# A two-layer diffusion backbone on one core: Fourier tables made first, and part of the adaLN of layer 0 moved from TensorE to VectorE

## The chip, the cores and the metric

The kernel runs on one core of one Trainium2 chip. A core has a matrix engine (TensorE, PE in the profile), VectorE (DVE), ScalarE (ACT), GpSimd (POOL) and SyncE (SP), which issues most DMAs. The metric is device time in microseconds for one execution; of several runs the median is given.

## What is computed

Two layers over 256 latent tokens and 256 context tokens with 1024 channels, all in float32. Layer 0 mixes tokens with a Conformer convolution module, layer 1 with a bidirectional mLSTM; each is followed by a squared-ReLU MLP. What concerns the change is the adaLN map, which makes shift, scale and gate vectors from the conditioning vectors, and the convolution module:

```python
sh1, sc1, g1, sh2, sc2, g2 = jnp.split(jax.nn.silu(c) @ ada_w[i] + ada_b[i], 6, axis=-1)   # and so for c_ctx
u = h * (1 + sc1) + sh1
a = u @ w_pw1 + b_pw1
a = a[..., :CONV_DIM] * jax.nn.sigmoid(a[..., CONV_DIM:])
a = dwconv(a, w_dw)                       # 31 taps; rows of 64 for the latent tokens
a = jax.nn.silu(layer_norm(a + b_dw, ln_g, ln_b))
y = a @ w_pw2 + b_pw2
h = layer_norm(ALPHA * h + g1 * y, ln1_g, ln1_b)
h = layer_norm(ALPHA * h + g2 * mlp(h * (1 + sc2) + sh2), ln2_g, ln2_b)
```

## The kernel before

Every float32 product is made of three matmuls of split halves: a weight is cast by ACT to a high part `wh` (line 154) and DVE subtracts it from the raw weight to get the low part `wl` (line 155); PE then does `wh*xh` (L177), `wh*xl` (L180) and `wl*xh` (L181). Weights come as 1 MB loads into `raw`, which has three buffers, all issued by SP in one queue. A PSUM tile named `mm` has three buffers, `cv` and `ln` two, `fl` one.

The order of instructions in each engine's queue is set by a scheduler when the program is built, from the order of the code and its own costs; only the start loop is pinned (`pin[0]`): there PE's instructions keep the order of the code.

The stages up to the first MLP:

- Start (`start0`, `start1`, `start2`): for each of 8 channel tiles, one load of the part of `ada_w` that makes shift and scale, a tile of `x` and a tile of pw1's weights. PE multiplies the conditioning vectors with the load (`ada_mm`, L297, into `fl`), DVE copies the result (L532), PE folds four partial sums (L305, into `ln`), DVE makes `sh1` and `sc1` (L537, L538), ACT and DVE make `u`, and PE adds this channel tile's share to the first four output tiles of pw1.
- Fourier tables: the depthwise convolution is done by products with cosine and sine tables `tab`, made by DVE with a polynomial (L583 to L600), then by PE with the 31 taps (L622) into `Hc` and `Hs`. In the code this stands behind the start loop; the scratch tiles `F` (five buffers) are shared with it.
- pw1: two output tiles for each group of weights (`gemm`), 24 matmuls each. Behind each tile `pw1_epi` takes the sigmoid on ACT, the gated product `E` on DVE (L673), four transposes on PE (L676) and a copy to `A` on ACT. After four channel tiles a pass of `spectral` follows (L691 or L696, then products with `Hc` and `Hs` on DVE, then L716), and so at the end.
- adaLN of layer 0: `Ada` makes the other vectors in units of 512 columns. One unit has two 1 MB loads and 8 matmuls (shown as 16 pieces of L297). Units 4 and 5 (g1) run beside pw1, units 6 to 9 (sh2 and sc2) behind it, units 10 and 11 (g2) in the MLP. `AdaRows` makes the vectors of layer 1 otherwise: DVE multiplies 128 rows of the transposed map with the conditioning vector `cb`, broadcast to all partitions, and sums each row (L357). It runs in the MLP of layer 0.
- `token_norm`: statistics, an inverse root by four Newton steps on one column (13 small DVE instructions), and two DVE passes, for each of four token tiles. `silu` then transposes (L775) and makes the input of pw2 for one stream; stream 0 is the context.

Of the kernel before, what the change touches and what calls it, by code (L numbers as in the profile page):

```python
# [72 lines left out]
def hybrid_kernel(ctx: ExitStack, tc: tile.TileContext, xT, vecs_d, cc_d, rows_d, wdw_d, ada0_w, ada_w, ada1_w, wg_d, pw1a, pw1, pw2, w1_0, w2_0,  # L73
# [216 lines left out]
    for i in range(2):  # L290
        nc.vector.tensor_tensor(cs[:, :, 14 + i], sgc[:, i * DT:(i + 1) * DT], cc[:, i * DT:(i + 1) * DT], op=ALU.mult)
    ada = [con.tile([P, 48, 2], F32, name=f"ada{l}") for l in range(2)]
# [48 lines left out]
    class AdaRows:  # L341

        def __init__(self, first, last):
            self.m, self.last = first, last

        def step(self):
            m = self.m
            if m == self.last:
                return
            self.m += 1  # L350
            if m % 2 == 0:
                self.raw = raw_load(ada1_w[m // 2])
            w = self.raw[:, m % 2 * D:(m % 2 + 1) * D]
            o = _OFF["ada_b1"][0] + m
            for s in range(2) if m < 2 * DT else (1,):
                dump = w if s else tp.tile([P, D], BF16, tag="F", name=nm("dump"), bufs=1)
                nc.vector.tensor_tensor_reduce(dump, w, cb[:, s, :], 1.0, vecs[:, o:o + 1], ALU.mult, ALU.add,  # L357
                                               accum_out=ada[1][:, m, s:s + 1])

        def flush(self):  # L360
            while self.m < self.last:
                self.step()
# [23 lines left out]
    HALVES_D = [slice(0, 512), slice(512, D)]  # L386
# [90 lines left out]
    def rsqrt(r, v, q):  # L477


        nc.vector.tensor_scalar(v, v, EPS, None, op0=ALU.add)  # L480
# [29 lines left out]
    U = maker(qa, "u", 3 * DT)  # L510
    padp = open_pool("pads")
    F = maker(padp, "F", 5)

    x, u = [], []
    KO0 = 4
    ps0 = [psum("cv" if m == 3 else "mm") for m in range(KO0)]
    sc1 = con.tile([P, 2, DT], F32, name="sc1p")
    sh1 = con.tile([P, 2, DT], F32, name="sh1p")
    o0 = _OFF["ada_b0"][0]
    st = {}  # L520

    def start0(f):
        t = X()
        raw = raw_load(ada0_w[f])
        nc.sync.dma_start(t, xT[f * P:(f + 1) * P, :])
        wr = F()
        nc.sync.dma_start(wr[:, :KO0 * P], pw1a[f])
        x.append(t)
        ps = psum("fl")[:, :2 * P]
        ada_mm(ps, [raw[:, kt * 2 * P:(kt + 1) * 2 * P] for kt in range(DT)])  # L530
        sb = F()[:, :2 * P]
        nc.vector.tensor_copy(sb, ps)  # L532
        st[f] = wr, sb

    def start1(f):
        tr = ada_fold(st[f][1], 2 * P, tag="ln")
        nc.vector.tensor_scalar(sh1[:, :, f], tr[:, 0:2], vecs[:, o0 + f:o0 + f + 1], None, op0=ALU.add)  # L537
        nc.vector.tensor_scalar(sc1[:, :, f], tr[:, 2:4], vecs[:, o0 + DT + f:o0 + DT + f + 1], 1.0,  # L538
                                op0=ALU.add, op1=ALU.add)
        u.append((U(F32R), U(F32R)))  # L540
        affine_split(*u[f], x[f], sc1, sh1, f)
        st[f] = split_w(st[f][0][:, 0:KO0 * P])

    def start2(f):
        for m in range(KO0):
            mm3(ps0[m], *kcol(st[f], m), *u[f], f == 0, f == DT - 1)

    pin[0] = Z.pin0
    for f in range(DT + 2):
        if 0 <= f - 1 < DT:  # L550
            start1(f - 1)
        if f < DT:
            start0(f)
        if f >= 2:
            start2(f - 2)
    pin[0] = False

# [55 lines left out]
    WIN = [[(F0[0:96, :], 0)], [(ge32, 0), (lt32, 1)], [(ge96, 0), (F0[0:96, :], 1)], [(ge32, 1)]]  # L613
    bdw = padp.tile([P, D], F32, name="bdw")
    nc.sync.dma_start(bdw, wdw_d[NTAP:NTAP + 1, :].broadcast_to([P, D]))
    Hc, Hs = [padp.tile([P, D], F32, name=n_) for n_ in ("Hc", "Hs")]
    for h_ in range(2):
        wd = F()[:NTAP, :]
        nc.sync.dma_start(wd, wdw_d[0:NTAP, h_ * 512:(h_ + 1) * 512])
        for t, w_ in ((Hc, WC), (Hs, WS)):  # L620
            ps = psum("ln")
            nc.tensor.matmul(ps, w_[:NTAP, :], wd, start=True, stop=True)  # L622
            nc.scalar.activation(t[:, h_ * 512:(h_ + 1) * 512], ps, AF.Identity, scale=cf)


# [34 lines left out]
    A = padp.tile([P, 4, D], F32, name="A")  # L660
    Y = [[U() for _ in range(2)] for _ in range(4)]
    bst = con.tile([P, 4, 2, 6], F32, name="bst")
    hold = {}

    def pw1_epi(m, ps):
        f, gate = m // 2, m % 2 == 0
        if gate:
            sg = tmp("E")
            nc.scalar.activation(sg, ps, AF.Sigmoid, bias=V("b_pw1", DT + f))
            hold[f] = sg  # L670
            return
        a = hold.pop(f)
        nc.vector.scalar_tensor_tensor(a, ps, V("b_pw1", f), a, op0=ALU.add, op1=ALU.mult)  # L673
        tr = psum("ln")
        for b in range(4):
            nc.tensor.transpose(tr[:, b * P:(b + 1) * P], a[:, b * P:(b + 1) * P], ident)  # L676
        nc.scalar.copy(A[:, :, f * P:(f + 1) * P], tr.rearrange("p (b c) -> p b c", b=4))
        if f % 4 == 3:
            for tt in range(4):
                spectral(f // 4, tt)  # L680

    def spectral(h, tt):

        sl = slice(h * 512, (h + 1) * 512)
        ps_ = []
        xfs = [psum() for _ in range(2)]
        for b in (1, 0):
            if tt < 2:
                w_ = WIN[2 * tt + b]
                for i, (fm, t) in enumerate(w_):  # L690
                    nc.tensor.matmul(xfs[b], fm, A[0:fm.shape[0], t, sl], start=i == 0, stop=i == len(w_) - 1)  # L691
            else:

                def fwd():
                    r = slice(64 * b, 64 * b + 64)
                    return nc.tensor.matmul(xfs[b], F0[r, :], A[r, tt, sl], start=True, stop=True,  # L696
                                            tile_position=(64 * b, 0))
                if b:
                    lead = fwd()
                else:  # L700
                    with tc.issue_after(lead.ins):
                        fwd()
        for xf in xfs[::-1]:
            p1, p2 = F(), F()
            nc.vector.tensor_tensor(p1, xf, Hc[:, sl], op=ALU.mult)
            nc.vector.tensor_tensor(p2, xf, Hs[:, sl], op=ALU.mult)
            ps_.insert(0, (p1, p2))


        o = psum("cv")  # L710
        for i, g_ in enumerate((G1, G2)):
            for b in (0, 1):
                r = 64 * b

                def inv():
                    return nc.tensor.matmul(o[r:r + 64, :], g_[:, r:r + 64], ps_[b][i], start=i == 0, stop=i == 1,  # L716
                                            tile_position=(0, r))
                if b == 0:
                    lead = inv()
                else:  # L720
                    with tc.issue_after(lead.ins):
                        inv()
        nc.vector.tensor_tensor(Y[tt][h], o, bdw[:, sl], op=ALU.add)
        nc.vector.bn_stats(bst[:, tt, h, :], Y[tt][h])
        if h == 1:
            token_norm(tt)

    def token_norm(tt):
        mv = con.tile([P, 4], F32, name=nm("mv"))
        nc.vector.bn_aggr(mv[:, 0:2], bst[:, tt].rearrange("p h c -> p (h c)"))  # L730
        ve, r, q = mv[:, 1:2], mv[:, 2:3], mv[:, 3:4]
        rsqrt(r, ve, q)
        nc.vector.scalar_tensor_tensor(q, mv[:, 0:1], -1.0, r, op0=ALU.mult, op1=ALU.mult)
        for h in range(2):
            nc.vector.tensor_scalar(Y[tt][h], Y[tt][h], r, q, op0=ALU.mult, op1=ALU.add)

    pre2 = {}

    def pre_pw2(g):
        raw = raw_load(pw2[g, 0])  # L740
        for m in (0, 1):
            pre2[2 * g + m] = split_w(raw[:, m * 1024:(m + 1) * 1024])

    for m in range(KO0):
        pw1_epi(m, ps0[m])
    ada_g1, ada_s2 = Ada(4, 2), Ada(6, 4)
# [39 lines left out]
    for _ in silu(0):  # L786
        pass
# [899 lines left out]
```

## Time and profile before

| | |
|---|---|
| Median of 3 runs | 1714.17 us (1712.07 to 1720.13) |
| The profiled execution | 1711.55 us, its span 1709.7 us |
| PE busy | 1678.7 us, 98% of the span |
| DVE busy | 1051.9 us, 62% |
| ACT busy | 734.1 us, 43% |
| Bytes moved by DMA | 301.65 MB, on average 176 GB/s |

The page is of one profiled execution; times in its views are microseconds from the start of the span. In rows of the timeline the two numbers are start and duration, and a bracket gives how long the engine had been idle and what ended that. In rows of groups they are count, busy time and mean, then idle time before. A matmul of 512 columns is shown longer than the time to the next, because matmuls are pipelined and their ends are modelled.

### The profile page before, as it was taken

How to read it: one execution, taken by the hardware profiler on the slowest of the kernel's cores; microseconds unless marked ns; L12 is line 12 of the kernel's file. 1: busy time of each engine (PE TensorE's matmuls, PEld its weight loads, DVE VectorE, ACT ScalarE, POOL GpSimd, SP SyncE). 2: the span in 40 equal slices, each digit the busy share in tenths (PEclk: the TensorE clock that was granted, in tenths of full speed). 3: DMA queues.
4: the chain of work that ended last, by engine and by line, in shares of the span. 5: the costliest groups of instructions: out<-in, count | busy, mean ns of one | idle time of the engine just before them, and what ended most of it. 6: DMA issues, size and time to landing. Idle time of an engine off the chain costs nothing.

```text
span 1709.7 us, 23961 instructions
## 1 busy us (share of the span) xinstructions
PE 1678.7 (98%) x9514; PEld 1401.4 (82%) x9514; DVE 1051.9 (62%) x1899; ACT 734.1 (43%) x1168; POOL 33.6 (2%) x84
## 2 busy tenths in 40 slices
PE   8999999999999999999999999999999999999998
PEld 5655798888888999987678899998867778888886
DVE  5556897975666786773132443343387786678765
ACT  3311763232324365543232433342276674555651
POOL 0000000000000000000000000000011110000000
PEclk9999999999999999999999999999999999999999
DMA  9323533655555145568663542353355555656651
GB/s 365 131 119 110 214 146 124 245 203 167 197 212 169 64 136 191 179 193 266 232 217 123 196 163 83 112 185 124 123 186 188 206 173 203 243 182 222 236 187 46
DMA packets 62687, 301.65 MB, mean 176 GB/s; under 512 B 8114, under 2 KB 22962, under 8 KB 29168
## 3 DMA queue, kind: packets, MB, share of 16 engines
q1 hardware_dynamic: 42832, 285.44, 47.3%
q10 hardware_dynamic: 19744, 14.69, 2.7%
q8 instruction: 75, 1.23, 0.3%
q14 instruction: 36, 0.29, 0.1%
HBM read 284.37 MB, written 15.74 MB: 176 GB/s over the span
## 4 chain that ended last, share of the span: by engine, by line
PE 87%; DVE 5%; DMA 4%; ACT 2%; issue 1%; POOL 0%; SPq 0%; DVEq 0%; ACTq 0%; POOLq 0%
PE mm L177 17%; PE mm L181 17%; PE mm L180 17%; DMA raw<-ada_w 3%; PE mm L187 3%; PE mm L185 3%; PE mm L1509 3%; PE mm L186 3%; PE cv L186 2%; PE cv L185 2%; PE cv L187 2%; PE mm L1510 2%; DVE wl L155 1%; PE fl L297 1%; PE fl L647 1%
## 5 line engine op out<-in xcount | busy, mean ns | idle before, releaser
L155 DVE TENSOR_TENSOR wl<-raw,wh 128x1024 fp32r<-128x1024 f32 x346 | 421.9, 1223 | 346.6 <-ACT wh L154 344.2
L154 ACT CAST wh<-raw 128x1024 fp32r<-128x1024 f32 x346 | 360.7, 1050 | 546.3 <-PE mm L180 350.1
L180 PE MATMUL mm<-u,wh 128*128 128x256 f32 (+1 forms) x1152 | 377.4, 328 | 0.0
L177 PE MATMUL mm<-u,wh 128*128 128x256 f32 (+1 forms) x1024 | 328.3, 321 | 5.8 <-DVE E L673 2.9
L181 PE MATMUL mm<-u,wl 128*128 128x256 f32 (+1 forms) x1024 | 327.3, 320 | 0.1
L180 PEld LDWEIGHTS mm<-u,wh 128*128 128x128 f32 x1152 | 220.6, 192 | 18.3 <-DVE mv L482 0.8
L177 PEld LDWEIGHTS mm<-u,wh 128*128 128x128 f32 x1024 | 196.3, 192 | 27.6 <-issue 8.9
L181 PEld LDWEIGHTS mm<-u,wl 128*128 128x128 f32 x1024 | 196.7, 192 | 15.8 <-DVE wl L155 1.6
L177 PE MATMUL mm<-xm,wh 128*128 128x512 f32 x256 | 102.8, 402 | 0.0
L185 PE MATMUL mm<-wh,xl 128*128 128x512 f32 x256 | 101.3, 397 | 0.7 <-ACT wh L154 0.5
L186 PE MATMUL mm<-wh,xl 128*128 128x512 f32 x256 | 100.4, 392 | 0.6 <-DVE xl L155 0.6
L181 PE MATMUL mm<-xm,wl 128*128 128x512 f32 x256 | 100.3, 392 | 0.0
L187 PE MATMUL mm<-wl,xl 128*128 128x512 f32 x256 | 99.7, 395 | 0.3 <-DVE wl L155 0.2
L177 PE MATMUL mm<-hid,wh 128*128 128x512 f32 (+1 forms) x256 | 93.3, 365 | 1.2 <-ACT hid L154 1.2
L180 PE MATMUL mm<-hid,wh 128*128 128x512 f32 (+1 forms) x256 | 93.0, 363 | 0.4 <-DVE hid L155 0.4
L181 PE MATMUL mm<-hid,wl 128*128 128x512 f32 (+1 forms) x256 | 92.9, 363 | 0.0
L357 DVE CUSTOM_DVE_ANT_0 raw<-raw,cb,vecs 128x1024 f32<-128x1024 f32 x48 | 61.1, 1281 | 33.5 <-DMA raw<-ada_w 33.2
L1509 PE MATMUL mm<-x,wh 128*128 128x512 f32 x224 | 79.0, 397 | 0.0
L180 PE MATMUL mm<-qq,wh 128*128 128x272 f32 x256 | 73.9, 289 | 0.0
L177 PE MATMUL mm<-qq,wh 128*128 128x272 f32 x256 | 73.9, 289 | 0.0
L181 PE MATMUL mm<-qq,wl 128*128 128x272 f32 x256 | 73.8, 288 | 0.0
L177 PEld LDWEIGHTS mm<-xm,wh 128*128 128x128 f32 x256 | 48.1, 188 | 22.5 <-issue 7.5
(481 smaller groups left out, 3102.4 us busy)
## 6 DMA issues: line engine op xcount, KB each, us to landing
raw<-w SPq DMA_DIRECT2D x64, 1024.0 KB, 4.9
raw<-ada_w SPq DMA_DIRECT2D x48, 1024.0 KB, 4.9
raw<-wo SPq DMA_DIRECT2D x32, 1024.0 KB, 4.8
raw<-wv SPq DMA_DIRECT2D x16, 1024.0 KB, 5.7
raw<-wqT SPq DMA_DIRECT2D x16, 1024.0 KB, 5.8
raw<-wq SPq DMA_DIRECT2D x16, 1024.0 KB, 5.1
raw<-wk SPq DMA_DIRECT2D x16, 1024.0 KB, 4.8
raw<-pw SPq DMA_DIRECT2D x10, 1024.0 KB, 6.5
```

The lines of the kernel that those rows point to most:

```text
L154: c = nc.scalar.copy(hi, src)
L155: nc.vector.tensor_tensor(lo, src, hi.bitcast(F32), op=ALU.subtract)
L177: a = nc.tensor.matmul(ps, wh, xh, start=start, stop=False)
L180: nc.tensor.matmul(ps, wh, xl, start=False, stop=False)
L181: nc.tensor.matmul(ps, wl, xh, start=False, stop=stop)
L185: nc.tensor.matmul(ps, xh, wh, start=start, stop=False)
L186: nc.tensor.matmul(ps, xl, wh, start=False, stop=False)
L187: nc.tensor.matmul(ps, xh, wl, start=False, stop=stop)
L297: a = nc.tensor.matmul(ps[32 * j:32 * j + 32], cs[:, kt, 14 - 2 * v:46 - 2 * v], blocks[kt], start=first and kt < 4, stop=last and kt >= 4 ...
L357: nc.vector.tensor_tensor_reduce(dump, w, cb[:, s, :], 1.0, vecs[:, o:o + 1], ALU.mult, ALU.add, accum_out=ada[1][:, m, s:s + 1])
L1509: a = lambda stop: nc.tensor.matmul(ps, wh, u2[kt], start=kt == 0, stop=stop)
L1510: b = lambda: nc.tensor.matmul(ps[:, LO], wl, u2[kt][:, LO], start=False, stop=False)
```

## The change

- The code of the Fourier tables stands ahead of the start loop. The taps' products (`taps`) are made in two halves, one early in pw1 and one at output tile 11 of pw1, into `Hcs` (four tiles of 512 columns instead of two of 1024).
- g1 and sc2 of layer 0 are made by `AdaRows(0, (2, 4))`: 16 column tiles of 128, two streams each, hence 32 row sums on DVE, one or two column tiles behind each pw1 tile. The units 4, 5, 8 and 9 of `Ada` go; units 6 and 7 (sh2) stay. The `ada_w` loads of these parts become loads of `adar_w`, the same bytes transposed.
- For the row sums `cb` is needed early. The two conditioning vectors, already on the chip as columns `cs`, are written to DRAM (`c_dr`) by two DMAs that ACT issues, and read back broadcast by SP. Before, `cb` was loaded from an input and passed through a sigmoid.
- `x` is scaled and `gb` added behind tile 5 of the loop instead of behind pw1.
- `token_norm` works on two token tiles: one inverse root of two columns, three Newton steps, and the norm is applied by ACT.
- In the second spectral pass the two context tiles, their norm, the first pw2 weights, the two remaining `Ada` units and `silu(0)` come ahead of the two latent tiles.
- `cb` and the later `hl` share one buffer, and the pool `adap` goes.

```diff
+    c_dr = dp.tile([2, D], F32, name="c_dr")
+    for i in range(2):
+        nc.scalar.dma_start(c_dr[i].rearrange("(f p) -> p f", p=P), cs[:, :, 14 + i])
...
+        def __init__(self, layer, parts):
+            self.l, self.todo = layer, [(layer * 6 + i) * DT + j for i in parts for j in range(DT)]
+
+        def step(self, n=1):
+            for _ in range(n):
+                if not self.todo:
+                    return
+                g = self.todo.pop(0)
+                if g % 2 == 0:
+                    self.raw = raw_load(adar_w[g // 2])
+                w, m = self.raw[:, g % 2 * D:(g % 2 + 1) * D], g - self.l * 6 * DT
+                o = _OFF[f"ada_b{self.l}"][0] + m
+                for s in range(2) if self.l == 0 or m < 2 * DT else (1,):
+                    dump = w if s else tp.tile([P, D], BF16, tag="F", name=nm("dump"), bufs=1)
+                    nc.vector.tensor_tensor_reduce(dump, w, cb[:, s, :], 1.0, vecs[:, o:o + 1], ALU.mult, ALU.add,
+                                                   accum_out=ada[self.l][:, m, s:s + 1])
...
-        nc.vector.tensor_scalar(v, v, 0.5, None, op0=ALU.mult)
-        for _ in range(4):
-            nc.vector.tensor_scalar(q, r, r, v, op0=ALU.mult, op1=ALU.mult)
+        for _ in range(3):
+            nc.vector.tensor_tensor(q, r, r, op=ALU.mult)
+            nc.vector.scalar_tensor_tensor(q, q, 0.5, v, op0=ALU.mult, op1=ALU.mult)
             nc.vector.scalar_tensor_tensor(r, q, -1.5, r, op0=ALU.add, op1=ALU.mult)
...
+    def token_norm(t0):
...
+        rsqrt(r, mv[:, :, 1], v, q)
+        nc.vector.tensor_tensor(z, mv[:, :, 0], r, op=ALU.mult)
+        nc.vector.tensor_scalar(r, r, -1.0, None, op0=ALU.mult)
+        for i in range(2):
+            for h in range(2):
+                y = Y[t0 + i][h]
+                nc.scalar.activation(y, y, AF.Identity, scale=r[:, i:i + 1], bias=z[:, i:i + 1])
...
-    ada_g1, ada_s2 = Ada(4, 2), Ada(6, 4)
+    ada0, ada_sh = AdaRows(0, (2, 4)), Ada(6, 2)
...
     def pw1_next(m, ps):
         pw1_epi(m + KO0, ps)
-        if m in Z.fd[:2]:
-            ada_g1.mm()
-        if m == Z.fd[2]:
-            ada_g1.end()
+        ada0.step(2 if m % 3 else 1)
+        if m == 5:
+            for s, sl in HALVES:
+                nc.vector.tensor_tensor(gb[:, s, :], ad(0, s, "g1"), VA("b_pw2"), op=ALU.mult)
+                for f in range(DT):
+                    nc.vector.tensor_scalar(x[f][:, sl], x[f][:, sl], ALPHA, gb[:, s, f:f + 1], op0=ALU.mult, op1=ALU.add)
+        if m == 7:
+            taps(1)
+
+    nc.sync.dma_start(cb, c_dr.rearrange("(o s) c -> o s c", o=1).broadcast_to([P, 2, D]))
...
-    gemm(pw1, range(6), u, T, pw1_next)
-    for g in range(2):
-        pre_pw2(g)
-    for i in range(4):
-        ada_s2.mm()
-    ada_s2.end()
+    for t0 in (0, 2):
+        for tt in (t0, t0 + 1):
+            spectral(1, tt)
+        token_norm(t0)
+        if t0 == 0:
+            for g in range(2):
+                pre_pw2(g)
+            for i in range(2):
+                ada_sh.mm()
+            ada_sh.end()
+            for _ in silu(0):
+                pass
```

What becomes of the queues shows best in three places. In each row stand the line, the operation, the tiles written and read with their numbers, and the shape.

First DVE at the start, around the copy of the first adaLN product out of `fl` (`fl_125` before, `fl_190` now). Before:

```order
L141 TENSOR_TENSOR fold<-fold,ident 128x16
L145 TENSOR_TENSOR foldg<-foldg,ident 128x16
L532 COPY F_134<-fl_125 128x256
L145 TENSOR_TENSOR foldg<-foldg,ident 128x16
L155 TENSOR_TENSOR wl_150<-F_123,wh_149 128x512
L145 TENSOR_TENSOR foldg<-foldg,ident 128x16
L537 TENSOR_SCALAR sh1p<-ln_136,vecs 128x2
```

The same place in the changed kernel, where `F_139`, `F_140`, `F_153` and `F_154` are the scratch tiles of the tables:

```order
L553 SCALAR_TENSOR_TENSOR F_139<-F_139,F_140 128x384
L550 TENSOR_TENSOR F_154<-tab 128x256
L554 SCALAR_TENSOR_TENSOR tab<-F_139,tab 128x384
L551 TENSOR_SCALAR F_153<-F_154 128x256
L586 COPY F_199<-fl_190 128x256
L553 SCALAR_TENSOR_TENSOR F_153<-F_153,F_154 128x256
L591 TENSOR_SCALAR sh1p<-ln_201,vecs 128x2
```

The copy stood behind small instructions on 16 columns; now nearly all of the table arithmetic stands ahead of it, and the rest between it and the instructions that follow.

Second DVE in the pw1 loop, up to the gated product of the second of two tiles ahead of the first spectral pass (`E_704`, now `E_715`). Before:

```order
L155 TENSOR_TENSOR wl_837<-raw_834,wh_836 128x1024
L673 SCALAR_TENSOR_TENSOR E_635<-mm_604,vecs,E_635 128x512
L155 TENSOR_TENSOR wl_867<-raw_834,wh_866 128x1024
L155 TENSOR_TENSOR wl_906<-raw_903,wh_905 128x1024
L673 SCALAR_TENSOR_TENSOR E_704<-mm_673,vecs,E_704 128x512
L155 TENSOR_TENSOR wl_950<-raw_903,wh_949 128x1024
```

Now, where an `ISA` row that reads `cb` is a row sum and the one behind it writes out its result:

```order
L155 TENSOR_TENSOR wl_846<-raw_843,wh_845 128x1024
L155 TENSOR_TENSOR wl_884<-raw_843,wh_883 128x1024
L360 ISA dump_877,ada_108<-raw_875,cb,vecs 128x1024
L360 ISA ada_108 128x1
L360 ISA raw_875,ada_108<-raw_875,cb,vecs 128x1024
L360 ISA ada_108 128x1
L360 ISA dump_880,ada_108<-raw_875,cb,vecs 128x1024
L360 ISA ada_108 128x1
L624 SCALAR_TENSOR_TENSOR E_715<-mm_684,vecs,E_715 128x512
```

Three row sums, on a load of their own (`raw_875`), now stand between the weights' low parts and the gated product.

Third PE behind the second spectral pass, where `cv` are the products of its last step, `u_576`, `u_578` (now `u_553`, `u_555`) the normalized context tokens and `fl_1290` the adaLN units. Before:

```order
L297 MATMUL fl_1290<-raw_1315,cs 32x512
L716 MATMUL cv_1247<-F_1243,tab 64x512
L716 MATMUL cv_1247<-F_1239,tab 64x512
L716 MATMUL cv_1247<-F_1244,tab 64x512
L716 MATMUL cv_1247<-F_1240,tab 64x512
L297 MATMUL fl_1290<-raw_1315,cs 32x512 x3
L775 MATMUL ln_1358<-ident,u_578 128x128
L775 MATMUL ln_1377<-ident,u_578 128x128
L297 MATMUL fl_1290<-raw_1317,cs 32x512 x4
```

Now:

```order
L667 MATMUL cv_1387<-F_1380,tab 64x512
L667 MATMUL cv_1406<-F_1402,tab 64x512
L667 MATMUL cv_1406<-F_1398,tab 64x512
L667 MATMUL cv_1406<-F_1403,tab 64x512
L667 MATMUL cv_1406<-F_1399,tab 64x512
L708 MATMUL ln_1299<-ident,u_553 128x128
L708 MATMUL ln_1318<-ident,u_553 128x128
L708 MATMUL ln_1299<-ident,u_555 128x128
```

The adaLN units no longer stand between the last spectral products and the context's transposes.

More of the change, by code (lines that the diff above doesn't have):

```diff
@@ L72, in hybrid_kernel @@
 @with_exitstack
[L73 removed]
+def hybrid_kernel(ctx: ExitStack, tc: tile.TileContext, xT, vecs_d, rows_d, wdw_d, ada0_w, ada_w, adar_w, wg_d, pw1a, pw1, pw2, w1_0, w2_0,
                   w1_1, w2_1, up_x, up_z, wv, wo, bo_d, wk, wq, wqT, wdown, out):
@@ L341, in hybrid_kernel @@
     class AdaRows:
[L343 to L358, printed above, removed]
+        def __init__(self, layer, parts):
[13 more added lines that the diff above has]
+                                                   accum_out=ada[self.l][:, m, s:s + 1])
         def flush(self):
-            while self.m < self.last:
-                self.step()
+            self.step(len(self.todo))
     def ad(l, s, which):
@@ L510, in hybrid_kernel @@
     U = maker(qa, "u", 3 * DT)
+    cb = xp.tile([P, 2 * D], F32, tag="hl", name="cb").rearrange("p (s c) -> p s c", s=2)
     padp = open_pool("pads")
     F = maker(padp, "F", 5)
[L514 to L556, printed above, removed]
     HL = L // 2
@@ L613, in hybrid_kernel, with start0 @@
     WIN = [[(F0[0:96, :], 0)], [(ge32, 0), (lt32, 1)], [(ge96, 0), (F0[0:96, :], 1)], [(ge32, 1)]]
+    x, u = [], []
+    KO0 = 4
+    ps0 = [psum("cv" if m == 3 else "mm") for m in range(KO0)]
+    sc1 = con.tile([P, 2, DT], F32, name="sc1p")
+    sh1 = con.tile([P, 2, DT], F32, name="sh1p")
+    o0 = _OFF["ada_b0"][0]
+    st = {}
+    def start0(f):
+        t = X()
+        raw = raw_load(ada0_w[f])
+        nc.sync.dma_start(t, xT[f * P:(f + 1) * P, :])
+        wr = F()
+        nc.sync.dma_start(wr[:, :KO0 * P], pw1a[f])
+        x.append(t)
+        ps = psum("fl")[:, :2 * P]
+        ada_mm(ps, [raw[:, kt * 2 * P:(kt + 1) * 2 * P] for kt in range(DT)])
+        sb = F()[:, :2 * P]
+        nc.vector.tensor_copy(sb, ps)
+        st[f] = wr, sb
@@ new lines, in hybrid_kernel, with pw1_epi @@
+    pin[0] = Z.pin0
+    for f in range(DT + 2):
+        if 0 <= f - 1 < DT:
+            start1(f - 1)
+        if f < DT:
+            start0(f)
+        if f >= 2:
+            start2(f - 2)
+    pin[0] = False
+    A = padp.tile([P, 4, D], F32, name="A")
+    Y = [[U() for _ in range(2)] for _ in range(4)]
+    bst = con.tile([P, 4, 2, 6], F32, name="bst")
+    hold = {}
+    def pw1_epi(m, ps):
+        f, gate = m // 2, m % 2 == 0
+        if gate:
+            sg = tmp("E")
+            nc.scalar.activation(sg, ps, AF.Sigmoid, bias=V("b_pw1", DT + f))
+            hold[f] = sg
+            return
+        a = hold.pop(f)
+        nc.vector.scalar_tensor_tensor(a, ps, V("b_pw1", f), a, op0=ALU.add, op1=ALU.mult)
+        tr = psum("ln")
+        for b in range(4):
+            nc.tensor.transpose(tr[:, b * P:(b + 1) * P], a[:, b * P:(b + 1) * P], ident)
+        nc.scalar.copy(A[:, :, f * P:(f + 1) * P], tr.rearrange("p (b c) -> p b c", b=4))
+        if f == 3:
+            for tt in range(4):
+                spectral(0, tt)
@@ L657, in wgq_step @@
                               qtr.rearrange("p (b j c) -> p j b c", b=4, j=4)[:, :, :, 0:16])
[L660 to L742, printed above, removed]
```

148 lines of the change are left out of this document (98 added, 50 removed).

## The prediction

> **What bounds the kernel now.** I read the page's engine table, then what TensorE waited for, then busy time by stretches of the first 300 us, because from the first MLP on both versions queue the same instructions in the same order.
>
> ```profile
> span 1709.7 us, 23961 instructions
> PE 1678.7 (98%) x9514; PEld 1401.4 (82%) x9514; DVE 1051.9 (62%) x1899; ACT 734.1 (43%) x1168; POOL 33.6 (2%) x84
> PE fl L297 <- DMA raw<-ada_w: 9.8, 4, 6.3
> PE mm L177 <- DVE E L673: 2.9, 1, 2.9
> ```
>
> TensorE (PE) is busy 98% of the span. A change can win only PE work taken out, PE waits removed (31 us in all), or stretches in which PE runs below its full clock; it loses wherever PE is made to wait. The two largest waits, in us, number of times and longest, lie where the change works. The stretches (span, busy us of PE, weight loads, VectorE (DVE), ScalarE (ACT), GpSimd; then granted PE clock, DMA share, GB/s):
>
> ```profile
> 0.00:10.00 10.00, 2.95 (x20) 1.61 (x20) 3.47 (x27) 3.88 (x8) 2.51 (x13) 1.00 0.82 311
> 47.30:83.30 36.00, 32.99 (x133) 22.18 (x131) 15.96 (x26) 12.14 (x16) 1.75 (x8) 0.91 0.33 120
> 170.00:180.00 10.00, 6.74 (x34) 2.07 (x34) 7.46 (x30) 2.08 (x5) 0.00 (x0) 1.00 0.89 352
> ```
>
> PE idles 7.05 us at the head, 3.0 us behind the Fourier tables, with the clock at 0.91 there, and 3.3 us at the end of the convolution.
>
> **Term A, tables in front: +6.8 us.** DVE's queue at the start and in the old place of the tables, then PE's at the start:
>
> ```profile
> 4.14 0.25 DVE L291 TENSOR_TENSOR cs<-sgc,vecs 128x8 f32<-128x8 f32 x2 [0.40 <-ACT sgc L289]
> 4.98 0.17 DVE L145 TENSOR_TENSOR foldg<-foldg,ident 128x16 f32<-128x16 f32 x1
> 8.28 0.43 DVE L532 COPY F<-fl 128x256 f32<-128x256 f32 x1 [3.13 <-PE fl L297]
> 9.81 0.22 DVE L537 TENSOR_SCALAR sh1p<-ln,vecs 128x2 f32<-128x2 f32 x1 [0.34 <-PE ln L305]
> 44.56 0.55 DVE L594 SCALAR_TENSOR_TENSOR F<-tab 128x384 f32<-128x384 f32 x1
> 50.24 0.28 DVE L597 TENSOR_SCALAR F<-F 128x256 f32<-128x256 f32 x1
> 52.09 0.41 DVE L599 SCALAR_TENSOR_TENSOR F<-F,F 128x256 f32<-128x256 f32 x1
> 6.29 1.93 PE L297 MATMUL fl<-raw,cs 128*32 128x256 f32 x16 [6.29 <-DMA raw<-ada_w]
> 8.76 1.01 PE L305 MATMUL ln<-fold,F 128*128 128x2 f32 x4 [0.54 <-DVE F L532]
> 13.96 1.93 PE L297 MATMUL fl<-raw,cs 128*32 128x256 f32 x16 [0.35 <-DMA raw<-ada_w]
> 15.83 0.80 PE L177 MATMUL mm<-u,wh 128*128 128x512 f32 x1
> ```
>
> From 44.56 to 50.24, the end of that instruction included, DVE does 17 instructions in 5.9 us, about 0.34 us each; the whole of the tables is about 10 us of DVE. DVE has 3.13 us free before the copy of the first adaLN result at 8.28, and its new queue puts some 30 instructions of tables and columns ahead of that copy. Counted on: the small operations end near 5.5, the fills and columns near 7.2, nineteen long ones at 0.34 to 0.47 near 14.2. So the copy is 5.9 us late. PE's queue at the start is fixed (product, fold, product, fold, product, first tile), so its fold and the second product wait too, at 14.7 and 15.7. Five more table instructions (0.34 each) lie between the copy and the second copy, of which about 0.9 us is not hidden by the wait from copy to L537 (1.53 us). The first tile starts at 22.6 instead of 15.83. From there PE has no gap, so nothing is caught up. Bounds: +4 (much of the tail hidden) to +8.
>
> **Term B, the old place of the tables: -7 us.**
>
> ```profile
> 47.09 0.39 PE L181 MATMUL cv<-u,wl 128*128 128x512 f32 x1
> 51.32 0.47 PE L177 MATMUL mm<-u,wh 128*128 128x512 f32 x1 [2.86 <-DVE E L673]
> 54.29 0.63 PE L177 MATMUL mm<-u,wh 128*128 128x512 f32 x1
> 58.30 3.88 PE L622 MATMUL ln<-F,tab 31*128 31x512 f32 x8
> 68.60 0.39 PE L177 MATMUL mm<-u,wh 128*128 128x512 f32 x1
> 68.82 0.39 PE L180 MATMUL mm<-u,wh 128*128 128x512 f32 x1
> 83.31 0.66 PE L676 MATMUL ln<-ident,E 128*128 128x128 f32 x4
> ```
>
> At full clock a 512 wide matmul starts every 0.228 us, so one tile of 24 takes 5.46. From 47.3 to 83.3 PE has four tiles (21.8), transposes (1.3), the taps L622 (3.9) and half an adaLN unit (1.0): 28.0 of 36.0 us, so 8.0 are lost. The stretch's row says 6.2: 3.0 idle and 0.09 of 36 at the lower clock. I take 7 of it, since the first 24 matmuls no longer wait for DVE's tables. The taps' products are now made in two halves; their work stays.
> The Trainium skill ("TensorE: Matmul & The Clock Gate", The HAM clock gate) says that after about 3.4 us with too little work the array's clock halves until about 3.4 us of work have passed; the trace agrees roughly: after 2.86 us without work a matmul lasts 0.63 instead of 0.39.
>
> **Term C, 32 row sums in the pw1 loop: +7 us.** One row sum and one weight load:
>
> ```profile
> 290.65 1.28 DVE L357 CUSTOM_DVE_ANT_0 raw<-raw,cb,vecs 128x1024 f32<-128x1024 f32 x1
> 291.86 0.08 DVE L357 DVE_READ_ACCUMULATOR2_ANT ada<- 128x1 f32 x1
> raw<-w SPq DMA_DIRECT2D x64, 1024.0 KB, 4.9
> ```
>
> A row sum takes DVE 1.21 us to the next instruction: 16 column tiles of two streams are 38.7 us in a loop of some 100 us. On average there is room; in the queue they stand ahead of instructions that PE needs. Counting from the end T of the start stage: four sums end at T+6.8 and only then free the buffer of the second pw1 group; its load lands at T+12.1 (4.9 us), its cast and subtraction end at T+14.3, where PE needs it at T+14.0. The gated product of tile 1 stands behind two sums and ends at T+17.4, its transposes are due at T+15.9: 1.5 us. Then three sums of a load that lands at T+25.3 stand ahead of the product of tile 3, which ends at T+29.6 though its tile is done at T+27.0: 2.7 us. One sum stands inside the first spectral pass: 1 us. After those gaps I charge 1.7 us of lower clock, by the matmuls at 54.29 (seven or eight at 0.2 more). Sum 6.9. In the second half of the loop the sums come when PE is not yet due. Bounds: 0, if loads land earlier, to +14, if each lateness moves the next load.
>
> **Term D, g1's two adaLN units off PE: -4.5 us.** By the chain's rows of one unit and of one closing fold:
>
> ```profile
> 236.65 1.85 PE fl L297 x16
> 126.50 0.79 PE fl L305 x8
> ```
>
> Two units at 1.85 and a fold at 0.79. The four units that leave PE (two here, two at the convolution's end) read 8 loads of 1 MB, and the row sums read 8 of 1 MB instead: no gain in bytes.
>
> **Term E, end of the convolution: -6 us.**
>
> ```profile
> 149.76 0.39 PE L181 MATMUL mm<-u,wl 128*128 128x512 f32 x1
> 173.23 1.04 PE L297 MATMUL fl<-raw,cs 128*32 128x512 f32 x2 [2.77 <-DMA raw<-ada_w]
> 179.40 0.62 PE L177 MATMUL mm<-u,wh 128*128 128x256 f32 x3 [0.46 <-ACT u L154]
> ```
>
> From the last pw1 matmul to the first of pw2 pass 29.6 us. Two units leave (3.7 of PE), and with them the wait of 2.77 for their load. The joint root replaces four chains of 13 small DVE instructions, and the norm's 8 DVE passes go to ACT, nearly idle there (2.08 of 10 us). I count the first product at 4.8, 16 products and their sums to 20, the norm on ACT to 22, the first pw2 matmul near 24. PE's saving cannot exceed 3.7 plus the waits of 2.77 and 0.46 and some tenths, 7.5; the latent half's norm, now behind ACT's eight casts of pw2's weights, may cost 1 to 2 of it. So -6, from -7.5 to 0.
>
> **Term F, c written element by element: +1 us.** ACT now writes two 4 KB vectors to DRAM during the start's loads. The only such writes in this trace come later: the issue, the one microsecond in which most of its packets went, and the ten after it:
>
> ```profile
> g_dr<-ada ACTq DMA_DIRECT2D x2, 4.0 KB, 14.3
> q10 hardware_dynamic: 891, 0.00, 50.1%
> DMA packets 34, 0.28 MB, mean 28 GB/s; under 512 B 0, under 2 KB 0, under 8 KB 0
> ```
>
> One vector is about 1024 packets; behind it loads ran at 28 GB/s for 10 us. In the start two vectors go, but between busy load packets, not in a burst, and PE is 6.8 us late anyway, so the loads have that lead. I take 1, from 0 to +11 (a 10 us stop each, less most of a 7 to 9 us lead).
> The Trainium skill ("DMA: Bandwidth & Descriptors", Rules for kernel authors) says that a strided last dimension becomes one descriptor per element, and it gives 512 B as the size below which a write is read, modified and written; the trace agrees with the count, and the stop fits.
>
> The removed sigmoids of c (4 ACT, 4 DVE of 0.6) lie beside PE without a wait: 0. The row-summed columns give g1 in time for the residual scaling, which no PE work waits for until pw2: 0.
>
> **Sum.** 6.8 - 7 + 7 - 4.5 - 6 + 1 = -2.7. The profiled execution took 1711.55 us, so 1708.9; the median of the runs shown is 2.6 higher, so 1711.
>
> **Rivals.**
> - Row sums cost PE nothing (DVE has idle time before most of its instructions in this loop) and the convolution's end wins its full 7.5: -2.7 - 7 - 1.5 - 1 = -12.2, 1702. Against it stands the queue's three sums ahead of tile 3's product.
> - Slower: the two element-wise writes stop the start's loads once for some 20 us, as the later one did for 10. With 8 us of lead 12 are PE's: -2.7 - 1 + 12 = +8.3, 1722. It decides when the writes pile up in a pause of the load queue instead of passing between its packets. For it speaks the 28 GB/s, against it that loads ran on while the first few packets went.
> - Each late sum delays the next group's load, and C doubles: 1718.
> - The tables aren't hidden and aren't late either, because the tail goes beside the waits for loads: A +4, 1708; inside the forecast.
> - By the clock gate's rule gaps of 1.5 and 2.7 us don't lower the clock; then C is 5.2 and the time 1709, also inside.
>
> **How the numbers follow.** About 0.5%, 8.6 us, is what a measurement tells from no change. The forecast (A to F within their middle) 0.60, the free row sums 0.22, the stopped loads 0.10, the doubled C 0.08. Faster by more than 0.5% needs under 1705.6: the 0.22 and a little of the forecast, 0.26; slower needs over 1722.8: 0.11; the rest 0.63. The range takes in the free sums with A's lower end, 1700, and the stopped loads, 1722. The forecast's own range is 1705 to 1718.
>
> **What would show it.** A: first tile at 22 to 23 us, PE waiting for the copy out of `fl`. B: no wait and full clock after the start stage but for the gaps of C. C: waits of PE's transposes for the gated product `E`, some 2 and 3 us. D and E: 64 fewer L297 pieces, pw2's first matmul 24 us after pw1's last. F: loads of the start that take over 10 us to land would make the prediction wrong on the slow side; a first tile at 18 us or no PE wait in the pw1 loop, on the fast side.

## The result, and the profile after

The changed kernel takes 1728.88 us (median of 5 runs, 1727.08 to 1729.94) against 1713.74 us before: a ratio of 1.0084 (95% interval 1.0069 to 1.0099), 15 us slower. The forecast was 1711, in a range of 1700 to 1722. The profiled execution took 1729.94 us with a span of 1727.9. Ratios here and below leave out the one execution in the slow state, at 2075.1 us in experiment 5, while medians keep it.

First the page's head, then what TensorE waited for in the whole span (line and tile, us in total, times, longest):

```profile
span 1727.9 us, 23850 instructions
PE 1672.3 (97%) x9442; PEld 1402.1 (81%) x9442; DVE 1082.4 (63%) x1927; ACT 737.5 (43%) x1172; POOL 33.4 (2%) x84
PE ln L308 <- DVE F L586: 20.5, 2, 14.1
PE fl L300 <- DMA raw<-ada_w: 6.5, 1, 6.5
PE ln L708 <- ACT S L712: 1.8, 2, 1.2
PE ln L708 <- ACT u L689: 1.6, 2, 1.0
```

TensorE has 72 matmuls fewer and is busy 6.4 us less, but it waits longer. The one large wait is for the copy of an adaLN product (`F`, L586) in the start stage, 14.1 us in one piece; there was none like it before. The time is best followed by a ledger: when TensorE reached the same five places, in us from the span's start, by the timelines of both (the fourth and fifth are the first 256 wide matmul of pw2 and the first 512 wide one of the MLP).

| | first tile | first spectral product | last pw1 matmul | first of pw2 | first MLP column tile | end |
|---|---|---|---|---|---|---|
| before | 15.83 | 84.87 | 149.76 | 179.40 | 276.76 | 1709.7 |
| after | 34.61 | 94.51 | 158.75 | 189.61 | 290.80 | 1727.9 |
| lag | +18.8 | +9.6 | +9.0 | +10.2 | +14.0 | +18.2 |

So 18.8 us are lost ahead of the first tile, 9.8 are won back up to the end of pw1, and 5 are lost again between there and the MLP. The 4 us of the rest lie in code that both versions queue alike; kernels below that also share it took 1431 to 1437 us for it in their profiled runs, so most of the 4 cannot be told from chance.

The head, in the changed kernel's trace: SyncE's queue and what it waited for in the first 40 us, the writes of `c`, two stretches (busy us of PE, weight loads, DVE, ACT, GpSimd; clock, DMA share, GB/s), then ACT, DVE and PE:

```profile
8.81 0.45 SPq L579 DMA_DIRECT2D x<-xT  x1
22.45 0.80 SPq L581 DMA_DIRECT2D F<-pw1a  x2
SPq L581 <- DMA c_dr<-cs: 13.1, 1, 13.1
SPq L579 <- DMA c_dr<-cs: 4.4, 1, 4.4
c_dr<-cs ACTq DMA_DIRECT2D x2, 4.0 KB, 20.5
20.00:22.00 2.00, 0.00 (x0) 0.00 (x0) 0.00 (x0) 0.00 (x0) 0.00 (x0) 1.00 0.00 0
22.00:24.00 2.00, 0.00 (x0) 0.00 (x0) 0.00 (x0) 0.00 (x0) 0.00 (x0) 1.00 0.00 0
30.07 0.62 ACT L154 CAST wh<-F 128x512 fp32r<-128x512 f32 x1 [12.41 <-DMA F<-pw1a]
30.73 0.69 DVE L155 TENSOR_TENSOR wl<-F,wh 128x512 fp32r<-128x512 f32 x1 [11.94 <-ACT wh L154]
31.33 0.42 DVE L586 COPY F<-fl 128x256 f32<-128x256 f32 x1
31.81 1.01 PE L308 MATMUL ln<-fold,F 128*128 128x2 f32 x4 [14.13 <-DVE F L586]
34.61 0.80 PE L177 MATMUL mm<-u,wh 128*128 128x512 f32 x1
```

Read upward from the last row: the first tile follows a fold, which waits for a copy, which stands in DVE's queue behind the subtraction of the first pw1 columns, which waits for their load. That load was issued at 22.45 only, after 13.1 us in which SyncE's queue waited for the first write of `c` to land; the two writes landed 18.0 and 22.9 us after their issue (20.5 in the row is the middle of the two). From 20 to 24 us nothing moves in the core's trace at all, DMA included. In the built program each transfer's completion is counted on one of eight semaphores in turn, and a load that is given the same one as an earlier transfer waits for that transfer's landing before it is issued: the first load of pw1's columns got the one of the first write, a load of `x` that of the second. The trace shows these waits, but not the semaphores; neither load reads what the writes wrote.

### The profile page after: what moved, and what is told of

Read it like the earlier page. It is cut to its first block, busy times and chain, and to the rows that moved or that the text cites. A ratio compares the mean times of both kernels' runs of the same rounds, so it can differ in the third digit from the quotient of the medians.

```text
span 1727.9 us, 23850 instructions
## 1 busy us (share of the span) xinstructions
PE 1672.3 (97%) x9442; PEld 1402.1 (81%) x9442; DVE 1082.4 (63%) x1927; ACT 737.5 (43%) x1172; POOL 33.4 (2%) x84
## 4 chain that ended last, share of the span: by engine, by line
PE 88%; DVE 5%; ACT 3%; DMA 3%; issue 1%; POOL 0%; DVEq 0%; ACTq 0%; POOLq 0%; SPq 0%
PE mm L177 18%; PE mm L181 18%; PE mm L180 18%; PE mm L1512 3%; PE mm L187 3%; PE mm L185 3%; PE mm L186 3%; PE mm L1513 2%; PE cv L187 2%; PE cv L186 2%; PE cv L185 2%; DVE wl L155 1%; DMA c_dr<-cs 1%; PE fl L773 1%; DMA raw<-w 1%
## 5 line engine op out<-in xcount | busy, mean ns | idle before, releaser
L181 PEld LDWEIGHTS mm<-u,wl 128*128 128x128 f32 x1024 | 196.9, 193 | 14.1 <-issue 1.3
L360 DVE CUSTOM_DVE_ANT_0 raw<-raw,cb,vecs 128x1024 f32<-128x1024 f32 x64 | 81.6, 1281 | 34.6 <-DMA raw<-adar_w 34.1
```

What stands on the lines that cost most here:

```text
L181: nc.tensor.matmul(ps, wl, xh, start=False, stop=stop)
```

## The experiments

Each kernel is compared with the kernel before on the same chip. On these chips the median of the kernel before lay between 1711.98 and 1715.23 us, so small differences between kernels of different experiments are read from the ratios. The edits are shown shortened. "Packed" below names the changed kernel with the first edit, on which most of the later ones stand.

**1. c in larger pieces.**

```diff
-    nc.scalar.dma_start(c_dr[i].rearrange("(f p) -> p f", p=P), cs[:, :, 14 + i])
+    # cq = sgc * cc, 128 x 16, contiguous; the columns of adar_w are permuted alike
+    nc.scalar.dma_start(c_dr[i].rearrange("(p f) -> p f", p=P), cq[:, i * DT:(i + 1) * DT])
```

> The changed kernel, with c written to DRAM as 128 pieces of 32 B for each vector instead of 1024 pieces of 4 B (the columns of the row-sum weights stand in the matching order; one small VectorE product more). Theory W: the first tile's loads stand in SyncE's queue behind loads that wait for the landing of c's element-wise writes (20.5 us in the trace of after, the DMA engines idle from 20 to 24 us). Then the writes land early, the first tile starts at 22 to 23 us instead of 34.6, and the time is 12 us lower: 1717, from 1714 to 1720. Rival T: the loads wait for the buffers that the tables hold, and the writes are bystanders: the first tile stays at 33 to 35 us and the time at 1729.

1714.44 us (ratio to before 1.0008, 0.9996 to 1.0020). What its two writes took, and its first tile:

```profile
c_dr<-cq ACTq DMA_DIRECT2D x2, 4.0 KB, 6.0
19.85 1.01 PE L310 MATMUL ln<-fold,F 128*128 128x2 f32 x4 [2.10 <-DVE F L588]
22.66 0.80 PE L177 MATMUL mm<-u,wh 128*128 128x512 f32 x1
```

The same bytes in 128 pieces for each vector land after 6.0 us instead of 20.5 (again the middle of two), the first tile is 12.0 us earlier and the time 14.4 lower. W holds, T falls: the tables alone put the first tile at 22.66, which is the sum of term A.

**2. The element-wise writes from GpSimd's queue** (`nc.scalar.dma_start` becomes `nc.gpsimd.dma_start`, nothing else).

> The changed kernel, with the two element-wise writes of c issued by GpSimd instead of ScalarE, so that no load of SyncE's queue shares a semaphore with them; still 1024 pieces of 4 B each. Theory W1 (what costs is that loads in SyncE's queue wait for the landing): loads go on, the first tile starts at 22 to 26 us, 1717 to 1721. Theory W2 (what costs is the pieces themselves, which hold the DMA engines): the loads are as slow as before, the first tile starts past 31 us, 1725 to 1731.

1724.55 us (1.0065, 1.0039 to 1.0090). The loads between 12 and 16 us, and the first tile:

```profile
12.00:14.00 2.00, 0.00 (x0) 0.00 (x0) 2.00 (x7) 0.00 (x0) 0.00 (x0) 1.00 0.12 13
14.00:16.00 2.00, 0.00 (x0) 0.00 (x0) 2.00 (x6) 0.00 (x0) 0.00 (x0) 1.00 0.21 17
30.73 0.80 PE L177 MATMUL mm<-u,wh 128*128 128x512 f32 x1
```

No load waits for a landing of `c` now, and yet loads run at 13 to 17 GB/s. Time and first tile lie between the two expectations, nearer to W2: of the 12 us at the first tile about 4 are gone and 8 are left. The edit does a second thing, though. GpSimd issues the writes until 6.63 and only then makes the index rows for the tables, so the copy of the first adaLN product runs at 16.76 instead of packed's 14.40; up to 2.4 of the 8 us may be that. How the loss splits with ScalarE's queue stays open, because GpSimd's queue is another path.

**3. The two writes alone, added to the kernel before** (the same two lines, read by nobody).

> The kernel before, with the two element-wise writes of c added and read by nobody. Theory W: the first tile stays near 16 us (its loads are issued ahead of those that wait), but a later load of the start stage waits for the landing and TensorE stops behind it: 10 to 15 us more, 1724 to 1729. Rival (the writes pass between the loads, as the prediction's term F had it): at most 2 us more, 1714 to 1716.

1728.35 us (1.0081, 1.0057 to 1.0105): as much as the whole change lost, from two writes of 4 KB. SyncE's queue in the first 50 us, then TensorE's first tile and its longest wait behind it:

```profile
SPq L530 <- DMA c_dr<-cs: 14.2, 1, 14.2
SPq L528 <- DMA c_dr<-cs: 4.1, 1, 4.1
19.72 0.80 PE L177 MATMUL mm<-u,wh 128*128 128x512 f32 x1
30.98 1.94 PE L300 MATMUL fl<-raw,cs 128*32 128x256 f32 x16 [6.84 <-DMA raw<-ada_w]
```

Since nobody reads `c_dr` here, the loads do not wait for its data. One part of W missed: the first tile did not stay near 16 us, because loads that were issued ahead of the waits also landed late. At pw1's last matmul the kernel is 13.6 us behind (163.33 against 149.76).

**4 and 5. The place of the tables.** In packed, the block of the tables goes back behind the start loop; and in the kernel before it goes in front of it, alone.

> The changed kernel with c in 32 B pieces, and the Fourier tables back behind the start stage as in the kernel before. By the ledger of the two traces the tables in front cost the first tile 6.8 us and win 8 to 9.3 us in the stretch after the start stage: this kernel's first tile is at 16 us, its wait behind the tables is back, and it takes 1 to 3 us more than the one with c in 32 B pieces alone: 1718 to 1720. Rival: the tables' place after the start stage costs little once the row sums stand there too (DVE is late anyway): 4 to 7 us less, 1710 to 1713.

> The kernel before, with the Fourier tables made ahead of the start stage and nothing else changed: terms A and B alone. As the prediction has them: the first tile starts at 22 to 23 us instead of 15.8, the wait of 2.9 us behind the tables goes, and the two cancel within 1 us: 1713 to 1715. Rival: A stands in full and B wins only its idle 3 us: 1717 to 1718.

packed_back took 1717.97 us (1.0018, 1.0002 to 1.0034), at the edge of the expectation, but its runs spread from 1711 to 1722 and reach over those of packed. before_tabs is the clean test: 1713.3 us (1.0001, 0.9991 to 1.0012). A and B cancel, as the prediction said: the first tile at 22.59 (A is +6.8), and from there to the first spectral product 60.8 us instead of 69.0 (B is -8.2).

**6. The row sums undone in packed** (g1 and the MLP's scale from four adaLN units; `x` is scaled behind tile 9 instead of 5).

```diff
-    ada0, ada_sh = AdaRows(0, (2, 4)), Ada(6, 2)
+    ada_g1, ada_sh = Ada(4, 2), Ada(6, 4)
-        ada0.step(2 if m % 3 else 1)
+        if m in Z.fd[:2]: ada_g1.mm()
+        if m == Z.fd[2]: ada_g1.end()
```

> The changed kernel with c in 32 B pieces, and the row sums undone: g1 and the MLP's scale come from four adaLN units on TensorE as before (two in the pw1 loop, two more at the convolution's end). If the row sums win what the units cost (two units and a fold in pw1, 4.5, and 3.7 at the end, less about 2 us of waits for the row sums): 1718 to 1721. Rival: VectorE's row sums cost TensorE as much in waits as the units in work: 1713 to 1715.

1716.77 us (1.0007, 0.9995 to 1.0020). The median lies between the two expectations, but the ratio is packed's 1.0008, so no gain of the row sums shows in the time. In the profiles the last pw1 matmul comes 2.7 us later with the first tile at the same 22.66; of the two further units at the convolution's end nothing is seen, because TensorE waits there anyway. What packed waits for between 60 and 150 us:

```profile
PE ln L629 <- DVE E L626: 1.4, 1, 1.4
PE mm L644 <- ACT A L630: 0.8, 1, 0.8
PE cv L669 <- DVE F L658: 0.5, 2, 0.2
```

**7 to 10. The end of the convolution.** Four kernels on packed. pk_filler writes the two adaLN units behind the context's SiLU; pk_norms keeps the new order and takes the old norm (a root for each tile, on VectorE); pk_oldend takes the old order and the old norm; pk_joint the old order with the new norm.

```diff
 # pk_filler
-            for i in range(2): ada_sh.mm()
-            ada_sh.end()
             for _ in silu(0): pass
+    for i in range(2): ada_sh.mm()
+    ada_sh.end()
 # pk_oldend; pk_joint has token_norm(tt - 1) after odd tt
-    for t0 in (0, 2):
-        for tt in (t0, t0 + 1): spectral(1, tt)
-        token_norm(t0)
+    for tt in range(4):
+        spectral(1, tt)
+        token_norm(tt)
```

> The changed kernel with c in 32 B pieces, and the two adaLN units at the convolution's end written behind the context's SiLU: in TensorE's queue they then stand behind the forward products of all four spectral pairs. Theory Q: the units and their copy and fold stand in the queues ahead of the second pair's products, hold these back by 3 to 4 us, and TensorE then idles behind the norm. Then from the last pw1 matmul to the first of pw2 pass 26 to 28 us instead of 30.6, and the time is 3 us lower, 1711 to 1712. Rival R (the joint root, which waits for two tiles and takes 7 us between other instructions, is the length of the end): 30 to 31 us, time 1714 to 1715.

> The changed kernel with c in 32 B pieces, and the token norm of the kernel before (a root for each tile, applied by VectorE), in the changed order of the queues. Theory Q (the place of the adaLN units costs): the time from the last pw1 matmul to the first of pw2 stays at 29.5 to 31 us, the time at 1713 to 1716. Rival R (the joint root costs): the first tile's norm is done 3 us sooner, 27 to 28 us, time 1711 to 1712.

> The changed kernel with c in 32 B pieces, and the convolution's end in the order and with the norm of the kernel before, with two adaLN units instead of four. By Q and R alike two units of 1.85 us and the wait for their load leave the 29.6 us of the kernel before: 25 to 27 us, and the pw2 stage after it is no longer slower than before: 1707 to 1710. Should it stay at 29 us or more, neither the order nor the norm made the end slow.

> The kernel with c in 32 B pieces and the order of the queues at the convolution's end as before, but with the joint root and the norm on ScalarE; against the 1709.3 of the one with the root for each tile on VectorE. Theory Q (only the place of the adaLN units cost time): 1708 to 1711, the stretch from last pw1 to first pw2 at 27 to 29 us, the pw2 stage at 96 to 98. Theory R (the joint root and its serial norm cost too): 1712 to 1715, the pw2 stage at 99 to 102 us with a lower clock in its first 10 us.

In this order: 1711.55, 1720.95, 1709.28 and 1712.92 us. By stages of the profiled runs (us), with the clock granted at the end and the ratio to before:

| | order, norm | last pw1 to first pw2 | clock there | from there to the MLP's column tile | both | ratio to before |
|---|---|---|---|---|---|---|
| before | old, old, four units | 29.6 | 1.00 | 97.4 | 127.0 | 1 |
| before_tabs | the same | 31.5 | 0.95 | 97.4 | 128.9 | 1.0001 |
| packed | new, new | 30.6 | 0.93 | 101.3 | 131.9 | 1.0008 |
| pk_filler | units last, new | 26.7 | 1.00 | 100.4 | 127.1 | 0.9978 |
| pk_norms | new, old | 28.3 | 0.94 | 108.4 | 136.8 | 1.0033 |
| pk_oldend | old, old | 28.7 | 1.00 | 96.5 | 125.2 | 0.9961 |
| pk_g (12) | the same | 30.2 | 0.89 | 96.5 | 126.7 | 0.9961 |
| pk_joint | old, new | 34.1 | 0.90 | 96.3 | 130.4 | 1.0002 |

Two pairs queue the same work at the end and show what one profile of it is worth: 29.6 and 31.5 us (32.5 in cw_before), 28.7 and 30.2, each time longer where less clock was granted. So 2 to 3 us at the end are not told from chance.

Q holds where it was tested alone: with the units last the end is 3.9 us shorter, of which the clock alone makes about 2, and the ratio is 0.9978 (0.9964 to 0.9991) against packed's 1.0008. R holds too, against my thinking that one of the two would do: in the old order the joint root makes the end 3.9 to 5.4 us longer (34.1 against 30.2 and 28.7) and the ratio 1.0002 (0.9994 to 1.0011) against 0.9961, though at the end itself and not in the pw2 stage as I wrote. pk_oldend missed its 25 to 27 us at the end: with two units fewer TensorE waits there instead, 1.7 us for `mv` and 1.0 for `S`. pk_norms is a miss for both theories: the end is shorter by 2.2, which may be chance, but VectorE, with the norm's passes back in its queue, is late for pw2 (3.6 us of waits for `hid`, 3.8 for `S`). How pk_joint waits, and its clock in the 10 us ahead of the first pw2 matmul:

```profile
PE ln L710 <- ACT u L691: 4.7, 2, 4.0
PE ln L710 <- ACT S L714: 3.7, 1, 3.7
174.50 5.75 ACT L691 ACTIVATE u<-u,mw 128x512 f32<-128x512 f32 x8 [0.87 <-DVE mw L687]
172.09:182.09 10.00, 2.07 (x6) 0.87 (x6) 5.61 (x27) 9.13 (x16) 0.00 (x0) 0.66 0.67 254
```

The root comes late for a pair, and then the norm of all four tiles, eight passes in 5.75 us, stands in ScalarE's queue ahead of the context's SiLU. VectorE's four passes for the context lay in the kernel before beside TensorE's units. pk_oldend is faster than the kernel before and than packed (ratio to before 0.9961, 0.9943 to 0.9979).

**11. Tables inside the start loop.** On pk_oldend; the block stands behind the loop's third step, with eight `F` buffers.

> c in 32 B pieces, the convolution's end of the kernel before (1709.3 us), and the Fourier tables written inside the start loop, behind its third step, with eight instead of five buffers for the pw1 columns and scratch. If VectorE's idle time in the start stage (3.5 of 10 us) takes the tables, the first tile starts at 16 us again and nothing waits after the start stage: 5 to 7 us less, 1702 to 1705. Rival: the tables stand ahead of copies and products that the start's tiles need, and TensorE waits there: 1708 to 1712.

1709.15 us (0.9980, 0.9968 to 0.9992), no gain over pk_oldend: the rival. The first tile starts at 15.95, but a later fold waits 4.5 us behind the tables:

```profile
PE ln L310 <- DVE F L535: 5.6, 3, 4.5
```

**12. The later element-wise writes.** On pk_oldend; the two gates of layer 1 are transposed and written in pieces of 512 B.

```diff
-        nc.scalar.dma_start(g_dr[i].rearrange("(f p) -> p f", p=P), ada[1][:, o:o + DT, 1])
+        nc.tensor.transpose(gt[0:DT, 0:P], ada[1][:, o:o + DT, 1], ident)
+        nc.vector.tensor_copy(gs[0:DT, 0:P], gt[0:DT, 0:P])
+        nc.scalar.dma_start(g_dr[i].rearrange("(f p) -> f p", p=P), gs[0:DT, 0:P])
```

> The kernel with c in 32 B pieces and the convolution's end of the kernel before (1709.3 us), and the two later element-wise writes (the gates of layer 1, 1024 pieces of 4 B each) turned into 8 pieces of 512 B each by a transpose. If the element-wise writes hold up loads there as they do in the start stage, the stops of about 10 us behind them go, and with them the wait of 1.6 us for the hidden activations near the end of the first MLP and its lower clock: 2 to 3 us less, 1706 to 1708. Rival: loads have lead enough there, or the wait has another cause: 1709 to 1710, the wait unchanged.

1708.64 us (0.9961, 0.9948 to 0.9974). TensorE's wait for the hidden activations, 300 to 700 us, the first two rows of pk_oldend and then of pk_g:

```profile
PE mm L177 <- DVE E L947: 2.5, 1, 2.5
PE mm L177 <- ACT hid L154: 1.6, 1, 1.6
```

```profile
PE mm L177 <- DVE E L947: 3.2, 1, 3.2
PE ln L971 <- DVE E L965: 0.3, 1, 0.3
```

The wait is gone. All thirteen other kernels have it, at 1.1 to 2.2 us, so it came from those writes. The ratio is that of pk_oldend: 1.6 us are too few to show, and the other wait grew by 0.7.

## Why the prediction was wrong

**The step that failed is F**, and with it the sign. I took +1 us, from 0 to +11; it measured +12.0 at the first tile and 14.4 in the time. The rows were there: 28 GB/s for 10 us behind such a write. Two thoughts were wrong. "Between busy load packets, not in a burst": pieces that pass one by one between the loads' packets are not cheap, they keep the write unfinished for as long as the loads run, and the loads themselves slow down beside them (270 and 143 GB/s from 10 to 12 and 12 to 14 us; packed 393 and 439). And I looked for its price at the DMA engines only, not in SyncE's queue, where later loads wait for the landing. The second rival had the stop and its price (12 us on TensorE), in part by luck: it made the stop depend on writes that pile up in a pause of the loads, and the trace shows them passing one by one between load packets. I gave it 0.10 for a reason, loads running on at first, that does not speak against it.

**A and B were right**: +6.8 and -7 forecast, +6.8 and -8.2 measured (before_tabs), the first tile at 22.6 to the tenth. (DVE's row count behind A was 16 instructions in 6.0 us, 0.37 each, not 17; nothing hung on it.)

**C was too dear; D was not measured alone.** Between the first tile and the last pw1 matmul before_tabs takes 126.7 us and packed 124.8: C and D together are -1.9, where +2.5 was forecast. With D at its 4.5, C is 2.6, which is about the sum of packed's three waits, 2.7; by pk_ada, where both are undone and pw1 ends 2.7 us later, C would be 1.8. Of the waits I had counted, those before tile 1 and tile 3 (1.5 and 2.7) became one of 1.4, and 0.8 for the spectral pass, and the granted clock stayed at 1.00 from 60 us to the end of pw1. Why the loads and sums came earlier than I had counted was not tried.

**E had the wrong sign**: -6 forecast, +4.9 measured (131.9 against 127.0, packed). Profiles with the old end (before, before_tabs, cw_before) took 127.0 to 129.9 us and those with the changed one (after, packed, poolq, packed_back) 130.8 to 132.1, so the size is +1 to +5. By before and packed about 1 us lies in the stretch that I forecast, up to the first pw2 matmul, and 4 in the pw2 stage, where I had allowed 1 to 2. Four parts of my sum were wrong. Two units do not leave that stretch: only three of the four stood in it, the fourth ran inside pw2, at 180.69 and 184.42. So 1.85 us could go there, not 3.7, and even that turned into waits: pk_ada has two units more at the end than packed, and its end is no longer. I let the 16 products run through to 20 us; in the queue the units' copy and closing sum stood between them, each behind TensorE. DVE in the changed kernel:

```profile
172.89 0.69 DVE L674 TENSOR_TENSOR u<-cv,bdw 128x512 f32<-128x512 f32 x1 [2.06 <-PE cv L667]
173.89 0.69 DVE L334 COPY F<-fl 128x512 f32<-128x512 f32 x1 [0.31 <-PE fl L300]
175.91 0.18 DVE L339 TENSOR_TENSOR ada<-fl,vecs 128x16 f32<-128x16 f32 x1 [0.73 <-PE fl L308]
176.12 0.64 DVE L656 TENSOR_TENSOR F<-mm,H 128x512 f32<-128x512 f32 x1
176.67 0.16 DVE L480 TENSOR_SCALAR mw<-mv 128x2 f32<-128x2 f32 x1
183.97 0.17 DVE L685 TENSOR_SCALAR mw<-mw 128x2 f32<-128x2 f32 x1
```

The products of the second pair of tiles begin at 176.1, 17.4 us after pw1's last matmul. The root then takes from 176.67 to 184.14, since nearly each of its small steps stands behind a product. And I charged nothing for the clock and too little for pw2 itself: behind the waits ahead of it TensorE is at 0.73 in its first 10 us (before: 1.00), 2.7 us, and in the whole stage it waits 3.4 us, where it waited 0.3.

```profile
189.61:199.61 10.00, 10.00 (x61) 9.74 (x62) 5.13 (x13) 7.74 (x18) 0.00 (x0) 0.73 0.00 0
179.40:189.40 10.00, 9.81 (x75) 7.38 (x76) 9.10 (x37) 7.37 (x17) 0.00 (x0) 1.00 0.95 369
```

**The sum** with the measured terms: 6.8 - 8.2 - 1.9 + 12.0 + 4.9 = +13.6, beside 15.1 in the medians; E's scatter alone makes it 10 to 14. My range ended at 1722 because it took F's stop as one case and kept E's full gain beside it.

## What to carry to other kernels

Count a transfer in pieces, not in bytes: two 4 KB writes in 4-byte pieces cost this kernel 15 us, and the same bytes in pieces of 32 B cost nothing that shows (first tile at 22.66, and at 22.59 in before_tabs, which does not write them). Ask of every write who waits for its landing, also loads that have nothing to do with it and share its semaphore or queue. And where work leaves an engine, follow the new queue of the engine that gets it, row by row, to the next instruction that TensorE needs: here the freed TensorE time went into waits and the slower clock behind them.

## What the runs showed of the hardware

The DMA queues of SyncE and ScalarE take turns piece by piece. Packets of the loads (q1) and of the writes of `c` (q10) in the changed kernel, in the microseconds from 10, 11 and 19:

```profile
q1 hardware_dynamic: 48, 0.39, 151.1%
q10 hardware_dynamic: 48, 0.00, 17.2%
...
q1 hardware_dynamic: 18, 0.15, 136.8%
q10 hardware_dynamic: 18, 0.00, 20.8%
...
q10 hardware_dynamic: 1105, 0.00, 62.2%
q1 hardware_dynamic: 28, 0.04, 10.0%
```

As long as loads are queued, one 4-byte piece goes for one packet of a load: from 8 to 18 us 602 pieces and 608 load packets. Only when the loads had run dry did 1105 go in one microsecond. The last pieces went by 20 us, and the loads that waited for the landings were issued at 22.45 and 27.71. The Trainium skill ("DMA: Bandwidth & Descriptors", Queues, rings and completion order) says that each DMA engine goes round its queues packet by packet; the equal counts agree. The same section of the Trainium skill puts typically 9 to 17 descriptors in a packet; here the counts are equal down to 18 in a microsecond, which looks like turns of single pieces. The same page of the Trainium skill (Anatomy of one DMA, which describes transfers issued by GpSimd) says that the completion follows only when the last write is confirmed, which can take long where the target is the chip's main memory; the 2 to 8 us between the last piece and the issues would fit that, though these writes were issued by ScalarE.
